# A hybrid decoder layer: each piece of side work is queued on ScalarE and VectorE behind the split of the weights beside it

## The chip, the cores and the metric

The kernel runs on one core of one Trainium2 chip. The metric is the device time of one execution in microseconds (us). The time before is the median of three executions. A profile of one further execution gives the rows that are read below. Engines are named as in the profile: PE is TensorE, ACT is ScalarE, DVE is VectorE, POOL is GpSimd, SP is SyncE, whose queue issues most of the DMAs. L268 is line 268 of the kernel.

## What is computed

One layer of a decoder on 512 tokens of width 1024, all in float32. After a modulated norm, three mixers (a Mamba-2 state space mixer called SSD, dilated window attention, and pooling over windows) are projected, gated, summed and projected again. An MLP with squared ReLU follows. Both have gated residuals. Cut to its frame:

```python
mod = (cond @ w_ada[l] + b_ada[l])[:, None, :]
sh1, sc1, g1, sh2, sc2, g2 = jnp.split(mod, 6, axis=-1)
h = _rms(x, norm1_w[l]) * (1 + sc1) + sh1
x = x + g1 * _hybrid_mixer(h, ...)
h = _rms(x, norm2_w[l]) * (1 + sc2) + sh2
x = x + g2 * (jnp.square(jax.nn.relu(h @ w_ff1[l])) @ w_ff2[l])
# in the mixer
z, xbc, dt_raw, q, k, v, u, gates = jnp.split(h @ w_in, splits, axis=-1)
# in _ssd, per head: the decay between two tokens of a chunk of 128
seg = a_cum[:, :, :, None] - a_cum[:, :, None, :]
decay = jnp.exp(jnp.where(causal, seg, -jnp.inf))
y_diag = jnp.einsum('bclsgj,bcsgjp->bclgjp', cb[..., None] * decay, X)
```

## The kernel before

*The stream of weights.* Each projection is a loop over tiles of weights, 128 x 1024 (two blocks of 128 rows of K, 512 KB). `wstream` loads a tile by a DMA on SP into `raw`. `wsplit` then makes two parts of it for float32 accuracy: ACT copies it to `wh` in a rounded format, DVE subtracts and keeps the rest in `wl`. `mm3` multiplies three times (L282 and L283 with wh, L284 with wl), for four accumulators `psacc` and two blocks, so a tile feeds 24 matmuls of 512 columns. `raw` has four buffers, `wh` and `wl` three each. Load and split are traced with high priority, 300 places ahead.

*Side work.* Everything that is not such a projection is cut into pieces. After each tile `tick()` takes one piece from the list `side`, and as many as `st["pace"]` says from the list `background`. Pieces of `side` are parts of the attention (scores, softmax, transposes: psqT, qT, pskT, kT, psS, p), of the SSD mixer (`ssd_steps`, `ssd_heads`), of the pooling (`win`, `pd`, psmix). `background` holds 32 pieces of `ada_later`: each loads a tile of `w_ada` on SP (wada, L243), multiplies and sums it on DVE (L244) and adds a bias (L245), for the later parts of `mod`. The pace is 0 until the loop over `w_ssd_out`, 2 there for its first round, then 1; the loads take one of four buffers in turn.

*Decay tiles.* For each pair of heads `ssd_heads` fetches two rows of `prow` into tiles `M`, spread over all partitions, by a DMA on SP (L899). Then come on ACT an exponential for `e` (L904), on DVE L911 or on ACT L909 the subtraction with a ReLU, on ACT the exponential L912, on DVE the product with `cb` (L913). In a later piece PE multiplies them into `psy` (L919), and DVE adds (L922, L928 to L933). Between the ReLU and exponentials on the one side and the SiLU of `conv` (L839) and of `z` (L321) or the square roots (L197) on the other, ACT loads a table.

*The order.* From L329 on, the instructions of DVE, ACT, PE and SP are put in order by a scheduler from the code's order and priorities, and by when it reckons that their inputs are ready. The order that comes out is fixed when the kernel is built. An engine then runs its own queue in that order and waits wherever an instruction's inputs are not there. `tc.issue_after(ins)` is a rule for the scheduler: what is traced within it comes, on the engine of `ins`, behind `ins`. It adds no wait between engines.

*PSUM.* Accumulators take banks that other results leave. The fourth accumulator of `take_x(1)` (psacc_3040, the XS projection of the second SSD group) gets the bank of `psst`, the state of an SSD chunk, which ACT copies to `prev` (L882). Copies of `z` (L321) come beside it.

Of the kernel before, what the change touches and what calls it, by code (L numbers as in the profile page):

```python
# [10 lines left out]
F32 = mybir.dt.float32  # L11
F32R = mybir.dt.float32r
AF = mybir.ActivationFunctionType
ALU = mybir.AluOpType
# [84 lines left out]
def kernel(ctx: ExitStack, tc: tile.TileContext, a: dict, out: bass.AP, dbg=None):  # L99
# [13 lines left out]
    def uid(s):  # L113
        cnt[0] += 1
        return f"{s}_{cnt[0]}"
# [47 lines left out]
    V, S = nc.vector, nc.scalar  # L163
# [75 lines left out]
    def ada_later(part, k):  # L239
        def go():  # L240
            o = modv[:, part - 2, k : k + 1]
            w = exp.tile([P, 2, T], F32, tag=("L0", "L1", "N0", "N1")[k % 4], name=uid("wada"))
            nc.sync.dma_start(w, a["w_ada"][part * 8 + k].rearrange("p (i t) -> p i t", i=2))  # L243
            V.scalar_tensor_tensor(w, w, 1.0, crow2, ALU.mult, ALU.mult, accum_out=o)  # L244
            V.tensor_tensor(o, o, vc("b_ada", part * 8 + k), ALU.add)  # L245
        return go


    background = [ada_later(part, k) for part in (2, 3, 4, 5) for k in range(8)]
    side, st = [], {}  # L250

    def tick():
        if side:
            side.pop(0)()
        for f in background[: st.get("pace", 0)]:
            f()
        del background[: st.get("pace", 0)]

    def flush():
        while side:  # L260
# [3 lines left out]
    def wsplit(raw, shape):  # L264
        wh = wsp.tile(shape, F32R, tag="wh", name=uid("wh"))
        wl = wsp.tile(shape, F32R, tag="wl", name=uid("wl"))
        S.copy(wh, raw)  # L267
        V.tensor_tensor(wl, raw, wh.bitcast(F32), ALU.subtract)  # L268
        return wh, wl

    def wstream(w, nk, ch, k0=0, ahead=None):
        for kp in range(nk // 2):
            with tc.high_priority(offset=AHEAD if ahead is None else ahead):
                raw = raws.tile([P, 2, T], F32, tag="raw", name=uid("raw"))
                nc.sync.dma_start(raw, w[ch, k0 // 2 + kp])
                wh, wl = wsplit(raw, [P, 2, T])
            for i in range(2):
                yield 2 * kp + i, wh[:, i, :], wl[:, i, :]
            tick()
# [696 lines left out]
    def pool_mix(gi):  # L976
        raw = raws.tile([P, 2, 256], F32, tag="raw", name=uid("wmix"))
        nc.sync.dma_start(raw, a["w_pool_mix"][gi])
        wh, wl = wsplit(raw, [P, 2, 256])
        for m in range(2):  # L980
            ps = psm("mix")
            cs = slice(m * P, (m + 1) * P)
            for k in range(2):
                mm3(ps, wh[:, k, cs], wl[:, k, cs], dh[2 * gi + k], dl[2 * gi + k], k == 0, k == 1)
            x, y = blk("poolh", F32R), blk("pooll", F32R)
            S.activation(x, ps, AF.Copy, scale=vc("pool_scale", gi * 2 + m))
            V.scalar_tensor_tensor(y, ps, vc("pool_scale", gi * 2 + m), x.bitcast(F32), ALU.mult, ALU.subtract)
            free(ps)
            ph_.append(x)
            pl_.append(y)  # L990
        free(*dh[2 * gi : 2 * gi + 2], *dl[2 * gi : 2 * gi + 2])
# [481 lines left out]
```

## Time and profile before

| | |
|---|---|
| median of 3 executions | 1100.88 us (1098.8 to 1102.0) |
| profiled execution | 1100.18 us, of which the span of the instructions 1098.4 us |
| mean granted TensorE clock | 0.998 |
| instructions | 14808 |
| read from HBM | 130.89 MB, 121 GB/s read and written over the span |

Busy time is counted per engine over the span. Engines work side by side, and PE is the one that is almost never idle; so the rows to read are those in which PE waits, with the engine that releases it, and then what that engine did before. A row of the timeline has the start, the duration, the engine, the line and the operation with its tiles, and in brackets the idle time ahead of it and who ended it. A row of groups has count, busy time, mean in ns, idle time ahead.

### The profile page before, as it was taken

Reading aid. Unit: us, or ns where it says so; the run is one execution under the profiler, and the core shown is the slowest. Engines: PE = TensorE matmul, PEld = TensorE weight load, DVE = VectorE, ACT = ScalarE, POOL = GpSimd, SP = SyncE. Lnnn points to the kernel's source line nnn. Section 1 sums busy time; section 2 is a strip of 40 time slices with the busy share of each in tenths; the row PEclk is TensorE's granted clock in tenths of the full one; section 3 lists DMA queues with packets and bytes.
Section 4 is the critical chain, followed back from the end, with each engine's and each line's share of the span. In section 5 each row is a group of like instructions: output and inputs, shape, how many; then the busy total and the mean of one; then the engine's idle time right before and its main releaser. Section 6 shows DMA issues by size and latency. Waiting matters only on the chain.

```text
span 1098.4 us, 14808 instructions
## 1 busy us (share of the span) xinstructions
PE 1087.7 (99%) x5806; PEld 928.4 (85%) x5806; DVE 709.0 (65%) x1287; ACT 520.2 (47%) x839; POOL 3.6 (0%) x10
## 2 busy tenths in 40 slices
PE   8999999999999999999999999999999999999998
PEld 7878888888887888887888888899889989989987
DVE  7955744461574658499984424477787587686664
ACT  8965865543793456424532123354344334334330
POOL 0000000000000000000000000000000000000000
PEclk9999999999999999999999999999999999999999
DMA  9823223222432233384283334260214234134032
GB/s 337 307 96 93 69 76 112 75 78 77 134 96 87 77 121 111 126 317 157 91 324 123 106 97 163 96 230 1 77 58 151 61 97 135 59 114 135 20 116 76
DMA packets 42057, 133.97 MB, mean 122 GB/s; under 512 B 4850, under 2 KB 5618, under 8 KB 41988
## 3 DMA queue, kind: packets, MB, share of 16 engines
q1 hardware_dynamic: 40784, 130.28, 35.8%
q0 software_dynamic: 480, 1.57, 0.5%
q10 hardware_dynamic: 724, 1.18, 0.3%
q8 instruction: 45, 0.74, 0.3%
q14 instruction: 24, 0.20, 0.1%
HBM read 130.89 MB, written 2.13 MB: 121 GB/s over the span
## 4 chain that ended last, share of the span: by engine, by line
PE 89%; DVE 5%; ACT 3%; DMA 2%; issue 1%; SPq 0%; DVEq 0%; ACTq 0%
PE psacc L282 22%; PE psacc L284 22%; PE psacc L283 22%; PE psacc L1334 11%; PE psacc L522 4%; PE psS L601 1%; DMA wada<-in_w_ada_dram 1%; DVE conv L837 1%; DMA M<-prow 1%; DVE win L964 1%; DVE wl L268 1%; PE pspT L698 1%; PE pskT L585 0%; PE pso L717 0%; PE psqT L580 0%
## 5 line engine op out<-in xcount | busy, mean ns | idle before, releaser
L268 DVE TENSOR_TENSOR wl<-raw,wh 128x1024 fp32r<-128x1024 f32 x140 | 171.0, 1223 | 206.0 <-ACT wh L267 205.6
L267 ACT CAST wh<-raw 128x1024 fp32r<-128x1024 f32 x140 | 146.6, 1048 | 264.9 <-PE psacc L283 192.5
L282 PE MATMUL psacc<-hl,wh 128*128 128x512 f32 x416 | 167.4, 402 | 3.1 <-ACT prev L882 2.0
L283 PE MATMUL psacc<-hh,wh 128*128 128x512 f32 x416 | 162.7, 391 | 0.0
L284 PE MATMUL psacc<-hh,wl 128*128 128x512 f32 x416 | 162.0, 391 | 0.0
L282 PE MATMUL psacc<-al,wh 128*128 128x512 f32 (+1 forms) x260 | 100.4, 386 | 0.0
L283 PE MATMUL psacc<-ah,wh 128*128 128x512 f32 (+1 forms) x260 | 100.4, 386 | 0.0
L284 PE MATMUL psacc<-ah,wl 128*128 128x512 f32 (+1 forms) x260 | 100.3, 386 | 0.0
L282 PEld LDWEIGHTS psacc<-hl,wh 128*128 128x128 f32 x416 | 78.6, 189 | 21.0 <-ACT prev L882 2.4
L283 PEld LDWEIGHTS psacc<-hh,wh 128*128 128x128 f32 x416 | 78.7, 189 | 17.0 <-issue 1.4
L284 PEld LDWEIGHTS psacc<-hh,wl 128*128 128x128 f32 x416 | 78.5, 189 | 16.9
L282 PE MATMUL psacc<-wl,rh 128*128 128x512 f32 x192 | 77.0, 402 | 0.0
L283 PE MATMUL psacc<-wh,rh 128*128 128x512 f32 x192 | 75.4, 393 | 0.0
L284 PE MATMUL psacc<-wh,rl 128*128 128x512 f32 x192 | 75.4, 393 | 0.0
L284 PEld LDWEIGHTS psacc<-ah,wl 128*128 128x128 f32 x260 | 48.8, 188 | 9.9
L282 PEld LDWEIGHTS psacc<-al,wh 128*128 128x128 f32 x260 | 48.9, 188 | 9.7
L283 PEld LDWEIGHTS psacc<-ah,wh 128*128 128x128 f32 x260 | 48.9, 188 | 9.6
L1394 DVE SCALAR_TENSOR_TENSOR xr<-psacc,modv,xr 128x512 f32<-128x512 f32 (+1 forms) x65 | 44.8, 741 | 18.7 <-PE psacc L284 18.7
L244 DVE SCALAR_TENSOR_TENSOR wada<-wada,crow 128x1024 f32<-128x1024 f32 x32 | 38.8, 1221 | 6.0 <-DMA wada<-in_w_ada_dram 6.0
L284 PEld LDWEIGHTS psacc<-wh,rl 128*128 128x128 f32 x192 | 36.1, 188 | 7.6
L282 PEld LDWEIGHTS psacc<-wl,rh 128*128 128x128 f32 x192 | 36.0, 188 | 7.2 <-ACT qT L581 0.2
L283 PEld LDWEIGHTS psacc<-wh,rh 128*128 128x128 f32 x192 | 36.1, 188 | 6.8
(407 smaller groups left out, 2344.2 us busy)
## 6 DMA issues: line engine op xcount, KB each, us to landing
raw<-in_w_in_dram SPq DMA_DIRECT2D x80, 512.0 KB, 3.5
raw<-in_w_ff_dram SPq DMA_DIRECT2D x52, 512.0 KB, 3.9
wada<-in_w_ada_dram SPq DMA_DIRECT2D x46, 512.0 KB, 5.1
rawl<-in_w_ff_dram SPq DMA_DIRECT2D x12, 512.0 KB, 3.4
wst<-in_w_in_dram SPq DMA_DIRECT2D x16, 256.0 KB, 7.8
M<-prow SPq DMA_DIRECT2D x16, 256.0 KB, 4.2
raw<-in_w_ssd_out_dram SPq DMA_DIRECT2D x8, 512.0 KB, 3.6
raw<-in_w_pool_out_dram SPq DMA_DIRECT2D x8, 512.0 KB, 3.5
```

The source lines that it names most:

```text
L244: V.scalar_tensor_tensor(w, w, 1.0, crow2, ALU.mult, ALU.mult, accum_out=o)
L267: S.copy(wh, raw)
L268: V.tensor_tensor(wl, raw, wh.bitcast(F32), ALU.subtract)
L282: mm(ps, lhsT=wh, rhs=xl, start=first, stop=False)
L283: mm(ps, lhsT=wh, rhs=xh, start=False, stop=False)
L284: mm(ps, lhsT=wl, rhs=xh, start=False, stop=last)
L522: mm(ps[j], lhsT=t[:, j, :], rhs=w, start=first, stop=last)
L601: mm(so[b], lhsT=qT[:, b * P : (b + 1) * P], rhs=kT[:, (b + 1) * P - n : (b + 1) * P], start=True, stop=True)
L698: nc.tensor.transpose(tp[:, i : i + P], pt[half][:, i : i + P], ident)
L837: V.scalar_tensor_tensor(t[:, i:], x[:, : T - i], cw[:, 3 - i, n : n + 1], t[:, i:], ALU.mult, ALU.add)
L1334: mm(o, lhsT=x[:, cs], rhs=y, start=first and k == 0 and j == 0 and n == 0, stop=k == 3 and n == 2, skip_group_check=True)
L1394: V.scalar_tensor_tensor(xT[d][:, ts], p[:, : ts.stop - ts.start], modv[:, 3, d : d + 1], xT[d][:, ts], ALU.mult, ALU.add)
```

## The change

`wsplit` now keeps in `edges` the two instructions of the latest split, the copy on ACT and the subtraction on DVE. `tick` traces its pieces within `issue_after` of both: on ACT they come behind the wh, on DVE behind the wl of the tile that was traced just before. What the pieces issue on PE and SP is not bound by this, except through the order that the scheduler finds. Pieces that `flush` runs are not bound. The decay rows are still loaded on SP's queue.

```diff
-    side, st = [], {}
+    side, st, edges = [], {}, []
 
     def tick():
-        if side:
-            side.pop(0)()
-        for f in background[: st.get("pace", 0)]:
-            f()
-        del background[: st.get("pace", 0)]
+        fs = side[:1] + background[: st.get("pace", 0)]
+        del side[:1], background[: st.get("pace", 0)]
+
+        with tc.issue_after(edges[0].ins), tc.issue_after(edges[1].ins):
+            for f in fs:
+                f()
...
-        S.copy(wh, raw)
-        V.tensor_tensor(wl, raw, wh.bitcast(F32), ALU.subtract)
+        edges[:] = S.copy(wh, raw), V.tensor_tensor(wl, raw, wh.bitcast(F32), ALU.subtract)
```

The split stands at L267 and L268 before, at L268 after. What moves, at three places:

ACT around the copies of z and prev, before. M_3374, M_3375 and M_4019 are decay tiles, the last one of the second SSD group:

```order
L912 ACTIVATE M_3374<-M_3374 128x512
L909 ACTIVATE M_3375<-M_3375,npc_939 128x128 x4
L912 ACTIVATE M_3375<-M_3375 128x512
L267 CAST wh_3087<-raw_3085 128x1024
L909 ACTIVATE M_4019<-M_4019,npc_939 128x128
L321 ACT_TABLE_LOAD
L321 ACTIVATE z_3029<-psacc_2869 128x512
L267 CAST wh_3129<-raw_3127 128x1024
L321 ACTIVATE z_3030<-psacc_2870 128x512
L321 ACTIVATE z_3031<-psacc_2871 128x512
L882 COPY prev_3027<-psst_3025 128x512
L321 ACTIVATE z_3032<-psacc_2872 128x512
```

and after, on the same engine:

```order
L268 CAST wh_3043<-raw_3041 128x1024
L851 COPY Bt_2933<-psBt_2935 128x512
L268 CAST wh_3087<-raw_3085 128x1024
L321 ACTIVATE z_3029<-psacc_2869 128x512
L321 ACTIVATE z_3030<-psacc_2870 128x512
L321 ACTIVATE z_3031<-psacc_2871 128x512
L268 CAST wh_3129<-raw_3127 128x1024
L321 ACTIVATE z_3032<-psacc_2872 128x512
L882 COPY prev_3027<-psst_3025 128x512
```

The decay tiles and the table load have gone from here: the first ones come behind wh_3229, two tiles later, and M_4019 in the next group's turn. On SP the DMA of M_4019 has moved from behind raw_3227 to behind raw_3736.

DVE between two products of psy (conv_3211 and conv_3217 are two of the SSD's outputs, wl_4384 the split of a tile of the pooling projection), one piece of the difference:

```order
 L268 TENSOR_TENSOR wl_4384<-raw_4381,wh_4383 128x1024
-L232 TENSOR_TENSOR sums_4111<-sums_4111,sq_4179 128x512
 L922 SCALAR_TENSOR_TENSOR conv_3211<-conv_3211,dcol_93,psy_4227 128x512
 L928 TENSOR_TENSOR e_4147<-psyo_4237,e_4147 128x384
-L245 TENSOR_TENSOR modv_94<-modv_94,vec_79 128x1
-L244 SCALAR_TENSOR_TENSOR wada_5139,modv_94<-wada_5139,crow_81 128x1024
 L930 TENSOR_TENSOR conv_3211<-conv_3211,e_4147 128x384
+L933 TENSOR_TENSOR conv_3211<-conv_3211,z_3480 128x512
```

The wada work has left this place; its first reduction (wada_4873) now stands right behind wl_4846, the first tile of `w_ssd_out`, and the last of the 32 follows one or two at a time behind later tiles.

ACT in the attention, before (qT_1232 and kT_1233 are the transposed q and k of one head, p_1177 and p_1178 the probabilities of the head before, rkr a root of the norm of k):

```order
L544 ACTIVATE sq_1215<-k_1200 128x512
L581 COPY qT_1232<-psqT_1234 128x512
L586 ACTIVATE kT_1233<-pskT_1240,qkw_282 128x512
L616 ACTIVATE p_1177,zs_182_748<-p_1177,nmx_749 128x128
L616 ACTIVATE p_1177,zs_182_748<-p_1177,nmx_749 128x256
L616 ACTIVATE p_1178,zs_182_748<-p_1178,nmx_749 128x256 x2
L197 ACT_TABLE_LOAD
L197 ACTIVATE rkr_1219<-ssk_1205,epsc_91 128x16
```

and after:

```order
L544 ACTIVATE sq_1215<-k_1200 128x512
L616 ACTIVATE p_1177,zs_182_748<-p_1177,nmx_749 128x128
L616 ACTIVATE p_1177,zs_182_748<-p_1177,nmx_749 128x256
L616 ACTIVATE p_1178,zs_182_748<-p_1178,nmx_749 128x256 x2
L197 ACT_TABLE_LOAD
L197 ACTIVATE rkr_1219<-ssk_1205,epsc_91 128x16
L581 COPY qT_1232<-psqT_1234 128x512
L586 ACTIVATE kT_1233<-pskT_1240,qkw_282 128x512
```

The two copies stand behind the exponentials and the root. PE has, ahead of the accumulator psacc_1291 that needs their banks, 18 matmuls of 512 columns and four transposes more than before.

## The prediction

> **What bounds the kernel now.** I read the busy shares first, then the waits of TensorE (PE), then the stretches around each wait.
>
> The first table of the page, and after it the list of what PE waited for (total, times, longest, us):
>
> ```profile
> PE 1087.7 (99%) x5806; PEld 928.4 (85%) x5806; DVE 709.0 (65%) x1287; ACT 520.2 (47%) x839; POOL 3.6 (0%) x10
> ```
> ```profile
> PE psacc L282 <- ACT prev L882: 2.0, 1, 2.0
> ...
> PE psacc L282 <- DVE conv L922: 0.9, 1, 0.9
> PE psmix L284 <- DVE wl L268: 0.4, 1, 0.4
> ```
>
> PE is busy 99% of 1098.4 us. The change adds and removes no matmul, so it can give back only PE's waits and what follows them. These three are the waits behind streamed weights; the list's others lie in the opening or are shorter, and no order changes there. Around the first, PE in order of time (start, duration):
>
> ```profile
> 333.78 0.38 PE L867 MATMUL psX<-cst,conv 128*128 128x128 f32 x2
> 334.00 1.02 PE L878 MATMUL psst<-Xd,Bt 128*128 128x512 f32 x2
> ...
> 336.47 0.39 PE L283 MATMUL psacc<-hh,wh 128*128 128x512 f32 x1
> 336.70 0.39 PE L284 MATMUL psacc<-hh,wl 128*128 128x512 f32 x1
> 339.11 0.79 PE L282 MATMUL psacc<-hl,wh 128*128 128x512 f32 x1 [2.02 <-ACT prev L882]
> ...
> 342.61 0.40 PE L284 MATMUL psacc<-hh,wl 128*128 128x512 f32 x1
> ```
> and the same time in windows (length; busy time of PE, PEld, DVE, ACT, POOL; granted clock, DMA share, GB/s):
> ```profile
> 336.90:339.10 2.20, 0.19 (x1) 0.00 (x0) 1.47 (x2) 2.20 (x5) 0.00 (x0) 1.00 0.00 0
> 339.10:342.50 3.40, 3.39 (x8) 2.72 (x9) 0.96 (x2) 0.46 (x1) 0.00 (x0) 0.50 0.48 154
> ```
>
> Full-speed matmuls start 0.23 us apart (336.47 to 336.70; 0.227 over longer rows of them). The gap from 336.70 to 339.11 is 2.41, so 2.18 too long. Then the granted clock is 0.50 for 3.4 us: eight intervals from 339.11 to 342.61 take 3.50 where 8 x 0.227 = 1.82 would do, 1.68 more. This one wait cost 3.86 us, twice what the list of waits shows.
>
> Why prev was late stands on ACT, with the DMA that it waited for:
>
> ```profile
> 330.85 0.33 SPq L899 DMA_DIRECT2D M<-prow  x1
> ```
> ```profile
> 334.35 0.40 ACT L909 ACTIVATE M<-M,npc 128x128 f32<-128x128 f32 x1 [3.32 <-DMA M<-prow]
> 334.77 1.28 ACT L321 ACT_TABLE_LOAD   x1
> 336.06 0.60 ACT L321 ACTIVATE z<-psacc 128x512 f32<-128x512 f32 x1
> 336.56 1.04 ACT L267 CAST wh<-raw 128x1024 fp32r<-128x1024 f32 x1
> 337.49 1.09 ACT L321 ACTIVATE z<-psacc 128x512 f32<-128x512 f32 x2
> 338.46 0.60 ACT L882 COPY prev<-psst 128x512 f32<-128x512 f32 x1
> ```
>
> A relu of the next group's decay tile (M_4019) had been put ahead of z and prev. Its row was fetched only at 330.85, so ACT stood 3.32 us, then loaded a table for 1.28, and prev ended at 339.06. PE's fourth accumulator needs the bank that prev reads. That piece of side work, pulled ahead of the main path, is what the change forbids.
>
> **The change, part by part.**
>
> *First wait.* In the new order ACT has, after the Bt copy, wh_3087, three z, wh_3129, the fourth z and prev, with no decay work and no table load between. PE finished the last z bank before its L867 of 333.78, so wh_3129 and the fourth z can run from there: 1.04 (the wh of 336.56), z 0.60 and prev 0.60, each overlapping the next by some 0.1, end near 335.8. prev also needs PE's psst, done at 335.02, which allows that. PE wants the bank at 336.70 + 0.23 = 336.93, 1.1 us later. I take the whole wait as gone, and the slow clock with it: **-3.86**. The bounds are 0, if something else holds ACT there, and -3.86.
>
> *Second and third waits.* On PE, on ACT (one wh) and on DVE:
>
> ```profile
> 497.62 0.39 PE L283 MATMUL psacc<-hh,wh 128*128 128x512 f32 x1
> 498.94 0.51 PE L282 MATMUL psacc<-hl,wh 128*128 128x512 f32 x1 [0.94 <-DVE conv L922]
> ...
> 535.36 0.50 PE L284 MATMUL psmix<-pdh,wl 128*128 128x512 f32 x1 [0.40 <-DVE wl L268]
> ```
> ```profile
> 493.44 1.05 ACT L267 CAST wh<-raw 128x1024 fp32r<-128x1024 f32 x1
> ```
> ```profile
> 498.14 0.75 DVE L922 SCALAR_TENSOR_TENSOR conv<-conv,dcol,psy 128x512 f32<-128x512 f32 x1
> ...
> 534.62 0.68 DVE L268 TENSOR_TENSOR wl<-wmix,wh 128x512 fp32r<-128x512 f32 x1
> ```
>
> 498.94 - 497.62 = 1.32, less 0.23, is 1.09 lost; here the clock stays. DVE's groups from 466 to 498.2 say who is in the way, and the windows how full it is:
>
> ```profile
> L244 DVE SCALAR_TENSOR_TENSOR wada<-wada,crow 128x1024 f32<-128x1024 f32 x11 | 13.4, 1223 | 2.4 <-DMA wada<-in_w_ada_dram 2.4
> L268 DVE TENSOR_TENSOR wl<-raw,wh 128x1024 fp32r<-128x1024 f32 x5 | 6.1, 1222 | 0.0
> ```
> ```profile
> 283.00:340.00 57.00, 54.98 (x264) 45.62 (x263) 39.90 (x64) 51.80 (x82) 0.00 (x0) 0.99 0.38 112
> 340.00:466.00 126.00, 126.00 (x621) 102.14 (x621) 74.26 (x119) 59.71 (x91) 0.00 (x0) 0.99 0.33 107
> 466.00:536.00 70.00, 68.67 (x364) 55.70 (x363) 67.03 (x150) 24.77 (x35) 0.00 (x0) 1.00 0.55 188
> 536.00:640.00 104.00, 104.00 (x461) 86.12 (x460) 63.77 (x106) 33.48 (x42) 0.00 (x0) 1.00 0.53 178
> ```
>
> DVE is busy 67.0 of 70 us from 466 to 536, and eleven wada reductions with their loads took 13.4 + 2.4 = 15.8 of the 32 us until the wait. All these now stand behind a split of w_ssd_out or later, after 540. The scheduler fills part of the room with pooling work, and conv L922 stays behind wl_4431, whose wh comes only when PE frees its slot. By the rows: wh ends at 494.49, a pooling add of 0.69 may be under way until 495.1, wl 1.22 and L922 0.75 less the overlap give 497.0; PE, which has three matmuls fewer ahead of that bank, arrives 0.68 earlier than 497.62 + 0.23, at 497.2. I take **-0.9** of 1.09 (bounds 0 and -1.09). The third wait lost 0.4 in the list and, with the slowed intervals beside it, up to 0.67. wl_4662 now comes some 3 us earlier on DVE, but PE too asks earlier, since fewer matmuls are put ahead of psmix L284: ready 531.6, asked 531.6, by the same kind of sum, no better than 1 us either way. I take **-0.4** (bounds +0.3 and -0.67).
>
> *Where the moved work goes.* The decay tiles leave 283 to 340 (ACT 51.8 of 57 busy) for 352 to 388, in the stretch with ACT 59.7 of 126 and DVE 74.3 of 126. psy needs the first and the third pair at (PE, then two wh on ACT):
>
> ```profile
> 374.17 1.09 PE L919 MATMUL psy<-M,X 128*64 128x128 f32 x16
> ...
> 388.92 1.09 PE L919 MATMUL psy<-M,X 128*64 128x128 f32 x16
> ```
> ```profile
> 350.98 1.05 ACT L267 CAST wh<-raw 128x1024 fp32r<-128x1024 f32 x1 [5.73 <-PE psacc L283]
> ...
> 381.42 1.04 ACT L267 CAST wh<-raw 128x1024 fp32r<-128x1024 f32 x1 [1.77 <-PE psacc L283]
> ```
> The pieces start on ACT behind the wh of 350.98 and, with the row durations of 0.39 to 0.63 an activation and 1.28 a table load, I get the first pair ready at 357.5, needed at 374.2; the third, behind the wh of 381.42, at 383.2, needed at 388.9, the tightest of the four. Cover 5.7 us: **0**. If it is gone, psy is late next. The 32 wada loads and reductions spread over 540 to 690, two for each weight tile of 24 x 0.227 = 5.45 us of PE. DVE has 63.8 of 104 busy there including 15 of them. A tile then asks DVE for 1.22 + 2 x (1.22 + 0.15) = 4.0 of 5.45, and wl is finished one or two tiles before PE asks: **0**. On SP's queue a wada load behind a raw load can wait for its slot and hold the next raw, which has four buffers ahead: **0**. POOL's queue is unchanged.
>
> *In attention*, at 116 to 125, side work gave way to other orders: the copies qT_1232 and kT_1233 stand behind four exponentials, a table load and a square root instead of before them.
>
> ```profile
> 118.90 0.60 ACT L581 COPY qT<-psqT 128x512 f32<-128x512 f32 x1
> 119.36 0.72 ACT L586 ACTIVATE kT<-pskT,qkw 128x512 f32<-128x512 f32 x1
> ...
> 122.30 1.28 ACT L197 ACT_TABLE_LOAD   x1
> 123.59 0.31 ACT L197 ACTIVATE rkr<-ssk,epsc 128x16 f32<-128x16 f32 x1
> ```
> I get them at 124.1 and 124.7. PE has 18 wide matmuls more ahead of them (18 x 0.227 = 4.1 us) and four transposes, and asks at 124.3 and 125.0 where it asked at 119.92. The margin is 0.2: bounds 0 and +1.3 (one table load), taken **+0.2**. Other places where orders changed (a da chain at 88 us, a bank at 392) have margins of 0.3 to 0.5 and may cost as much: together **+0.3**, bounds 0 and +1.
>
> [...]
>
> Sum: -3.86 - 0.9 - 0.4 + 0.2 + 0.3 = **-4.7**. The profiled execution took 1100.18 (span 1098.4 and 1.8 around it), so 1095.5 on its scale; the median of the runs shown is 1100.88, 0.7 higher. I take **1096.0**, between 1095.5 and 1096.2.
>
> **The rivals.** *Only the first wait goes.* Then -3.86 and +0.5: 1097.1 to 1097.5, about 1097.3. For it: both later waits are on DVE with margins of 0.2 or none. Against: eleven reductions leave.
>
> *New waits in attention or at a bank eat the gain.* A wait of 2 us, as at 336.7, costs 3.9 with its clock: 1096.0 + 3.9 = 1099.9, the same within the measurement (0.3%, 3.3 us, is about the least that timing tells from no change). For it: margins of 0.2 to 0.5 us. Against: the wait must pass about 1 us before the clock falls, since after the 0.94 at 498.94 it did not.
>
> *The slow clock stays.* If the 0.50 at 339.1 had another cause than the wait, 1.68 stays: 1097.7. [...] The trace shows the fall right behind 2.2 us idle, and nowhere else in this stretch.
>
> *Slower: the decay tiles come late.* Their pieces sit in ACT's order behind a wh that itself waits for PE (1.77 at 381.42). If the third pair is over 5.7 us later than I sum, PE waits at psy, at 388.9, and the fourth pair follows. At 3 us each with 1.7 of slow clock that is 9.4: 1096.0 + 9.4 = 1105.4. For it: extra table loads between z's silu and relu and exp. Against: ACT and DVE are half empty there.
>
> *The change does not bind here*, since a scheduler puts other work ahead of prev: 1100.9. The order shows prev without such work, so this is small.
>
> **How the numbers follow.** Forecast 0.57 (1094.8 to 1097.2); only the first wait 0.13; slow clock stays 0.05; attention or a bank 0.12; no effect 0.05; slower 0.08. Faster by over 0.3% means under 1097.6: the first, most of the second and half of the third, 0.70. Slower, above 1104.2: 0.08. The rest, 0.22. The range reaches from 1094.0 (all bounds at their best, -5.6, with 0.5 of scatter) to 1099.9, where the slower case and the unchanged one are left out.
>
> **What would show it.** Right: no PE wait on prev L882 and a clock of 1.00 around 339; PE's total of waits on conv L922 and wl L268 under 0.4; no relu of M between 283 and 340; wada reductions up to about 690 us without PE waits on wl. Wrong: a PE wait on qT L581 or kT L586 near 124, on M L913 at psy, or another window with clock 0.50.

## The result, and the profile after

The change makes the kernel faster by about half a per cent: 1093.55 us in the median (1093.37 to 1094.08, 6 executions) against 1099.59 of the kernel before beside it (1096.67 to 1102.0, 6), a ratio of 0.9945 with a 95% interval of 0.9930 to 0.9961. The profiled execution took 1093.54 with a span of 1091.7 and a mean granted clock of 1.0. Forecast were 1096.0 and a range of 1094.0 to 1099.9: the sign was right, and the time lies 0.45 below the range. One later execution of the kernel before, in the third group below, took 1819.69 us at a mean clock of 0.556 and is left out of all figures.

The page after, PE's busy time and the chain that ended last (shares of the span by engine), and then all that PE waited for (total, times, longest, us):

```profile
PE 1085.3 (99%) x5806; PEld 927.7 (85%) x5806; DVE 711.9 (65%) x1287; ACT 514.9 (47%) x835; POOL 3.6 (0%) x10
...
PE 98%; DVE 1%; DMA 0%; issue 0%; ACT 0%; SPq 0%; DVEq 0%
```
```profile
PE pssx L400 <- DVE sq L409: 1.3, 1, 1.3
PE pswarm L393 <- DVE ones L362: 1.1, 1, 1.1
PE psrx L454 <- DVE diag L451: 0.3, 1, 0.3
```

The list of waits no longer has prev, conv and wl; the three that are left lie in the opening. The stretches of the prediction, after (length; busy time of PE, PEld, DVE, ACT, POOL; clock, DMA share, GB/s):

```profile
283.00:340.00 57.00, 57.00 (x278) 47.55 (x277) 31.92 (x41) 28.57 (x41) 0.00 (x0) 1.00 0.35 116
340.00:466.00 126.00, 126.00 (x625) 102.23 (x624) 81.32 (x141) 79.24 (x129) 0.00 (x0) 1.00 0.36 115
466.00:536.00 70.00, 70.00 (x371) 57.38 (x370) 57.88 (x119) 29.04 (x43) 0.00 (x0) 1.00 0.23 74
536.00:640.00 104.00, 104.00 (x461) 86.11 (x460) 71.58 (x124) 31.74 (x39) 0.00 (x0) 1.00 0.71 242
```

PE is busy all the time in all four. ACT fell from 51.8 to 28.6 us in the first and rose from 59.7 to 79.2 in the second: the decay tiles moved. DVE fell from 67.0 to 57.9 in the third and rose by 7.8 in the fourth: the wada work moved. At the first of the old waits, on ACT and then on PE:

```profile
332.60 1.04 ACT L268 CAST wh<-raw 128x1024 fp32r<-128x1024 f32 x1
333.55 0.59 ACT L321 ACTIVATE z<-psacc 128x512 f32<-128x512 f32 x1
334.08 0.59 ACT L882 COPY prev<-psst 128x512 f32<-128x512 f32 x1
```
```profile
335.94 0.39 PE L282 MATMUL psacc<-hl,wh 128*128 128x512 f32 x1
336.16 0.39 PE L283 MATMUL psacc<-hh,wh 128*128 128x512 f32 x1
```

prev ends at 334.67 and PE starts into that bank at 335.94, 1.27 us later, at full pace. At the second, DVE's addition and PE's first matmul into the bank, and at the third, DVE's split and PE's psmix:

```profile
491.18 0.74 DVE L922 SCALAR_TENSOR_TENSOR conv<-conv,dcol,psy 128x512 f32<-128x512 f32 x1
...
525.66 0.69 DVE L268 TENSOR_TENSOR wl<-wmix,wh 128x512 fp32r<-128x512 f32 x1
```
```profile
492.27 0.40 PE L282 MATMUL psacc<-hl,wh 128*128 128x512 f32 x1
...
526.55 0.40 PE L284 MATMUL psmix<-pdh,wl 128*128 128x512 f32 x1
```

L922 ends at 491.92, 0.35 before PE asks; wl ends at 526.35, 0.20 before. So the last two are met with little to spare.

To see where the time came from, the start of PE's k-th matmul was set against the k-th of the kernel before (both have 5806), at points where the order of the matmuls is the same in both. The differences, added up to some points of the kernel before:

| up to, us before | after minus before, us | this part |
|---|---|---|
| 20 (opening) | -0.57 | -0.57 |
| 116 | -0.47 | +0.10 |
| 220 (attention) | -0.94 | -0.47 |
| 296 | -0.98 | -0.04 |
| 348 (first wait) | -4.90 | -3.92 |
| 497 | -4.89 | 0.0 |
| 503 (second wait) | -6.16 | -1.27 |
| 543 (third wait) | -6.66 | -0.50 |
| end | -6.65 | 0.0 |

Nothing was given back after 116; the 0.10 up to there comes at 88 to 96, beside the da chain that the prediction names.

### The profile page after: what moved, and what is told of

Its sections match the earlier page's. It is cut to its first block, busy times and chain, and to the rows that moved or that the text cites. A ratio compares the mean times of both kernels' runs of the same rounds, so it can differ in the third digit from the quotient of the medians.

```text
span 1091.7 us, 14800 instructions
## 1 busy us (share of the span) xinstructions
PE 1085.3 (99%) x5806; PEld 927.7 (85%) x5806; DVE 711.9 (65%) x1287; ACT 514.9 (47%) x835; POOL 3.6 (0%) x10
## 3 DMA queue, kind: packets, MB, share of 16 engines
HBM read 130.89 MB, written 2.13 MB: 122 GB/s over the span
## 4 chain that ended last, share of the span: by engine, by line
PE 98%; DVE 1%; DMA 0%; issue 0%; ACT 0%; SPq 0%; DVEq 0%
PE psacc L282 25%; PE psacc L284 25%; PE psacc L283 25%; PE psacc L1334 11%; PE psacc L522 4%; PE psS L601 1%; PE psy L919 1%; PE pso L717 1%; PE psyo L927 1%; PE pspT L698 1%; PE pso L715 1%; PE psqT L580 0%; PE pskT L585 0%; PE psst L878 0%; DMA xT<-in_x_dram 0%; PE psmix L284 0%
## 5 line engine op out<-in xcount | busy, mean ns | idle before, releaser
L268 DVE TENSOR_TENSOR wl<-raw,wh 128x1024 fp32r<-128x1024 f32 x140 | 171.1, 1222 | 191.8 <-ACT wh L268 189.2
L268 ACT CAST wh<-raw 128x1024 fp32r<-128x1024 f32 x140 | 146.8, 1050 | 275.5 <-PE psacc L283 176.5
L1334 PE MATMUL psacc<-gh,wl 128*128 128x256 f32 x144 | 40.8, 283 | 0.0
```

The lines of the kernel that those rows point to most:

```text
L268: edges[:] = S.copy(wh, raw), V.tensor_tensor(wl, raw, wh.bitcast(F32), ALU.subtract)
L1334: mm(o, lhsT=x[:, cs], rhs=y, start=first and k == 0 and j == 0 and n == 0, stop=k == 3 and n == 2, skip_group_check=True)
```

## The experiments

The account to be tested: what stops PE is side work that stands in ACT's and DVE's order ahead of main work. On ACT it is the ReLU behind the late row M; on DVE it is the wada reductions. The rivals are that the relief comes from fewer table loads and less work on ACT, or that the slow clock is no result of the wait. Edits are to the kernel after. All times of a group come from one chip with runs of the kernel before beside them.

**One edge at a time.** First group: the kernel before took 1097.82 (1096.37 to 1099.6, 19 executions).

```diff
-        with tc.issue_after(edges[0].ins), tc.issue_after(edges[1].ins):
+        with tc.issue_after(edges[0].ins):   # e1: behind wh on ACT only
+        with tc.issue_after(edges[1].ins):   # e2: behind wl on DVE only
```

> The pieces are held behind the wh on ACT only, not behind the wl on DVE. The order on ACT at z and prev is that of the changed kernel, but eleven or so wada reductions stay on DVE ahead of conv L922. My account (three separate waits): the wait on prev with its slow clock is gone (-3.9 of the 6.0 us), the waits of DVE (1.3 and 0.5) may stay, so 1 to 2 us above the changed kernel: 1094.6 to 1095.4. Rival (DVE's queue is what matters): prev is late again or other waits of 2 us come, 1097 or more.

With ACT's edge alone: 1094.24 (1093.96 to 1094.64), ratio 0.9965 (0.9952 to 0.9978). That is 0.4 below the expected band: the wait for prev is gone, and so is the one for conv, which the expectation had let stay, though wada reductions still run on DVE from 465.8 (9 between 455 and 498 where the kernel before has 12). Only the third is left, PE's row:

```profile
529.36 0.50 PE L284 MATMUL psmix<-pdh,wl 128*128 128x512 f32 x1 [0.58 <-DVE wl L268]
```

> The pieces are held behind the wl on DVE only. On ACT decay work stays among z and conv, with 37 rows of table loads where the kernel before has 30 and the changed one 26; but the ReLU of M_4019 is gone from ahead of z, and wada is gone from DVE. My account: all three waits gone, within 0.5 us of the changed kernel: 1093.5 to 1094.1. Rival (the gain is ACT's saved table loads and load on ACT, 5 us fewer): 7 more loads of 1.28 make ACT late for z, prev or wh, 1097 to 1100.

With DVE's edge alone: 1094.49 (1093.97 to 1094.68), ratio 0.9963 (0.9950 to 0.9976), and no wait of PE after the opening. The median lies 0.4 above the end of the expected band; in the trace, the kernel after is ahead by 0.46 in the opening and by 0.38 between there and 220. ACT in this kernel, where decay work and table loads have stayed:

```profile
324.85 1.28 ACT L912 ACT_TABLE_LOAD   x1
326.15 0.63 ACT L912 ACTIVATE M<-M 128x512 f32<-128x512 f32 x1
327.56 1.05 ACT L268 CAST wh<-raw 128x1024 fp32r<-128x1024 f32 x1 [0.78 <-PE psacc L283]
328.62 1.28 ACT L321 ACT_TABLE_LOAD   x1
...
335.38 0.59 ACT L882 COPY prev<-psst 128x512 f32<-128x512 f32 x1
```
and the window over it:
```profile
283.00:340.00 57.00, 57.00 (x276) 47.53 (x275) 32.08 (x40) 49.23 (x77) 0.00 (x0) 1.00 0.39 116
```

ACT is busy 49.2 of 57 us, nearly as before (51.8), and prev is in time. So the table loads and the amount of work on ACT were not the cause; what is gone from here is the ReLU that waited for its row. Either edge alone gives most of the gain. That a decay piece uses both engines, so that one bound instruction puts the piece off, would explain it, but no run takes this apart.

**One kind of side work at a time.** In the same group:

```diff
-        fs = side[:1] + background[: st.get("pace", 0)]
+        fs, bs = side[:1], background[: st.get("pace", 0)]   # e4: only wada bound
...
+        for f in fs:
+            f()
         with tc.issue_after(edges[0].ins), tc.issue_after(edges[1].ins):
-            for f in fs:
+            for f in bs:
                 f()
```

> Only the background pieces (wada) are held, the side work is free as before. My account: the waits on conv L922 and wl L268 go (1.3 + 0.5), that on prev with its slow clock stays: 1.7 us below the kernel before, about 1098, with a PE wait on prev of about 2 us and a granted clock of 0.5 behind it. Rival (the first wait is also fed by DVE's crowding): the wait on prev shrinks, 1096 or less.

1096.08 (1095.78 to 1098.74, 10 executions), ratio 0.9987 (0.9978 to 0.9997). The wait for prev is back, those for conv and wl are not: the sums of differences fall by 1.26 and 0.50 across them, as in the whole change, and DVE is busy 20.0 of the 32 us from 466 to 498 (29.6 before). So binding the wada work alone takes away the second and third wait. The wait for prev, the windows on it, and one in the opening:

```profile
PE psacc L284 <- ACT prev L884: 1.6, 1, 1.6
```
```profile
10.00:15.00 5.00, 5.00 (x29) 5.00 (x29) 3.65 (x14) 2.60 (x6) 0.00 (x0) 0.59 1.04 365
...
338.70:340.70 2.00, 0.41 (x3) 0.03 (x1) 1.51 (x2) 2.00 (x5) 0.00 (x0) 1.00 0.00 0
340.70:344.20 3.50, 3.50 (x15) 2.85 (x16) 0.92 (x2) 0.45 (x2) 0.00 (x0) 1.00 0.44 150
```

After this wait of 1.59 the clock stays at 1.00. The profiled execution (1098.41) lost its 2 us in the opening instead, where the clock fell to 0.59; seven of the ten executions, with a clock of 0.999 and above, took 1095.8 to 1096.2. The 1098 that was expected counted on the slow clock and was missed; the time is near the rival's. But the wait is only 0.4 shorter than in the first profile, and in the kernel before no wada reduction runs on DVE between 52 and 463 us, so these can't have fed a wait at 337.

The other way round, only the decay pieces of the second SSD group are bound (e5):

```diff
-        side.append(lambda: next(gens[0]))
+        side.append(bind(lambda: next(gens[0])))   # bound only if g == 1
...
-            side.append(go)
+            side.append(bind(go))
```

> Only the decay pieces of the second SSD group are held; on ACT the one difference at prev is that the ReLU of M_4019 no longer stands ahead of z. My account (that one instruction, which waits for its DMA, makes the whole first loss): -3.9 us against the kernel before, 1095.5 to 1096, no PE wait on prev, waits on DVE as before. Rival (decay work of the first group and its table loads on ACT between 283 and 340 make prev late as well): a wait of 1 us or more on prev stays, 1097 to 1099.

1095.33 (1095.03 to 1097.16, 8), ratio 0.9976 (0.9966 to 0.9986). ACT, where the first group's decay work stands as before, but the ReLU of the second group doesn't stand ahead of z:

```profile
328.70 0.63 ACT L911 ACTIVATE M<-M 128x512 f32<-128x512 f32 x1
329.24 1.04 ACT L267 CAST wh<-raw 128x1024 fp32r<-128x1024 f32 x1
330.29 1.28 ACT L320 ACT_TABLE_LOAD   x1
...
334.72 0.59 ACT L881 COPY prev<-psst 128x512 f32<-128x512 f32 x1
```
and PE at the third wait:
```profile
530.22 0.50 PE L283 MATMUL psmix<-pdh,wl 128*128 128x512 f32 x1 [0.82 <-DVE wl L267]
```

Binding these pieces alone takes away the first wait: the sums of differences go from -0.73 to -4.65 across it, as in the whole change. The second wait went too, against the expectation and though the wada work is not bound. DVE has 8 reductions there instead of 12 between 455 and 498, the last at 485.8 where the kernel before has one at 492.8; later decay work seems to have taken their turns. It is no less busy for it (31.7 of the 32 us from 466 to 498; in e1, where the wait is gone as well, 31.5; before 29.6). The third wait grew to 0.82. So the first wait belongs to the pieces of this group, of which one ReLU stood ahead of z. The second and third go with the wada work by e4; in e1 and e5 the second hangs on which work has DVE's turns just ahead of L922, and not on how busy DVE is.

**Both kernels again, and the slow clock.** Second group, another chip: the kernel before took 1097.74 (1095.84 to 1101.27, 28 executions).

> The changed kernel once more, beside many executions of the kernel before on one chip. Account as it stands after the first four experiments: without the slow clock the first wait costs some 2, the others 1.3 and 0.5, attention 0.4, so 4.2 us between the medians (ratio 0.996). Rival (the 6.0 us of the first comparison is the usual gain, the slow clock usual too): ratio 0.9945.

The unchanged kernel after: 1093.51 (1093.3 to 1093.97, 6), ratio 0.9962 (0.9949 to 0.9975). That is the 4.2 us of the account, and the interval leaves out the rival's 0.9945.

> The kernel before once more, for a second profile of it and its scatter. If the slow clock behind the wait on prev is a matter of chance, most executions have a mean granted clock of 1.000 and lie within about 1 us of each other, and those with 0.998 or less lie about 1.7 us above them. If it always follows the wait, all have 0.998. Ratio 1.000.

The unchanged kernel before: 1097.82 (1096.69 to 1101.84, 10), ratio 0.9999 (0.9986 to 1.0011). Eight executions have a mean clock of 0.999 or above and lie between 1096.7 and 1097.9; two have less and took 1099.38 and 1101.84. The profiled one is the slowest. PE at both waits, and the windows:

```profile
336.05 0.39 PE L284 MATMUL psacc<-hh,wl 128*128 128x512 f32 x1
338.29 0.50 PE L282 MATMUL psacc<-hl,wh 128*128 128x512 f32 x1 [1.84 <-ACT prev L882]
...
499.05 0.65 PE L282 MATMUL psacc<-hl,wh 128*128 128x512 f32 x1 [1.82 <-DVE conv L922]
```
```profile
338.30:342.00 3.70, 3.70 (x10) 2.90 (x11) 0.93 (x2) 0.43 (x1) 0.00 (x0) 0.57 0.46 142
...
500.00:503.00 3.00, 3.00 (x9) 2.37 (x8) 3.00 (x8) 1.25 (x2) 0.00 (x0) 0.56 0.02 5
```
and DVE's addition:
```profile
498.25 0.74 DVE L922 SCALAR_TENSOR_TENSOR conv<-conv,dcol,psy 128x512 f32<-128x512 f32 x1
```

Here the clock fell behind both waits. L922 ends at 498.99, in the first profile at 498.89, although PE came 0.8 us earlier: DVE's own queue, with the wada loads that it waits for, sets that time in this kernel, so what PE had gained upstream came back as wait. Of 65 executions of the kernel before in the three groups, 10 show a mean clock of 0.998 or less, and they are its ten slowest (1099.35 and above); the twelve executions of the kernel after all show 1.0 and keep within 0.8 us. Both profiles of before fell on such executions. A usual one was not profiled, so what its waits look like was not seen.

To measure how long a wait brings the clock down, dummy activations that switch tables were put ahead of prev in the kernel after, and later matmuls were kept from filling the gap (`end` holds the last matmul of the projection's first block):

```diff
                     if d == 0:
+                        for f in (AF.Exp, AF.Sqrt) * 2 if g == 0 else ():   # e6_tables6: * 3
+                            S.activation(pv[:, :1], sp[:, :1], f, scale=0.0)
                         S.copy(pv, sp)
...
+                    if ch == XS + 1 and k:
+                        es.enter_context(tc.issue_after(end[0].ins))
```

> The changed kernel with four extra one-column activations, each with a table load, on ACT ahead of the copy to prev, and with PE kept from taking the second block's matmuls of that projection before the fourth accumulator's first ones. prev is then some 5.9 us later; less 1.3 to spare and 1.9 of other matmuls put between, PE waits about 2.7. If the clock falls behind every wait of 2 us or more: about 4.4 above the changed kernel in every execution. If it falls by chance: 2.7 in some, 4.4 in others. [...]

1095.62 (1095.54 to 1095.97, 10), ratio 0.9982 (0.9973 to 0.9992), 2.1 over the kernel after. ACT, PE, and the window behind:

```profile
338.16 0.17 ACT L888 ACTIVATE prev<-psst 128x1 f32<-128x1 f32 x1
338.35 1.28 ACT L888 ACT_TABLE_LOAD   x1
339.64 0.17 ACT L888 ACTIVATE prev<-psst 128x1 f32<-128x1 f32 x1
```
```profile
340.49 0.50 PE L282 MATMUL psacc<-hl,wh 128*128 128x512 f32 x1 [1.51 <-ACT prev L889]
```
```profile
340.00:344.00 4.00, 3.51 (x15) 2.92 (x16) 2.76 (x4) 0.44 (x2) 0.00 (x0) 1.00 0.00 0
```

The wait is 1.51, where 2.7 was expected, so this run doesn't test a wait of 2 us. It leaves the clock at 1.00, in all ten executions (0.999 and above).

> The same with six such activations: a PE wait of about 5.7. [...] If the clock is a matter of chance even here, some executions at 5.7.

1100.72 (1100.04 to 1104.66, 10), ratio 1.0033 (1.0021 to 1.0044), 7.2 over the kernel after. PE's wait, and the window behind it:

```profile
343.76 0.71 PE L282 MATMUL psacc<-hl,wh 128*128 128x512 f32 x1 [4.47 <-ACT prev L889]
```
```profile
343.70:347.20 3.50, 3.44 (x8) 2.72 (x9) 2.76 (x4) 0.01 (x1) 0.00 (x0) 0.53 0.00 0
```

A wait of 4.47 (5.7 was expected) brings the clock to 0.53 for 3.5 us, and all ten executions show a mean clock of 0.998 or less. Two more table switches, 2 x 1.48 = 2.96 us by the rows above (338.16 to 339.64), cost 1100.72 - 1095.62 = 5.1: the window has eight matmuls in 3.5 us, like the eight intervals of 3.50 that the prediction read behind the wait for prev, so the clock adds some 1.7 by that estimate, and 0.4 stays unexplained. So with the same neighbours a wait of 1.51 leaves the clock at 1.00, and one of 4.47 brings it down to 0.53.

**Attention, and the spread of wada.** Third group: the kernel before took 1097.82 (1096.68 to 1100.74, 8 executions). Here the binding begins with the SSD part, after the attention (e9):

```diff
-        with tc.issue_after(edges[0].ins), tc.issue_after(edges[1].ins):
+        with ExitStack() as es:
+            for e in edges if st.get("bind") else ():
+                es.enter_context(tc.issue_after(e.ins))
...
+    st["bind"] = True
     ps = evac(gemm_feat(w_in, 8, BCC, hh, hl), "xc")
```

> The changed kernel, with pieces held only from the first projection of the SSD mixer (BCC) on; in the attention the old order stands. Account: all of the gain but the 0.4 us that four profiles with held side work show between 116 and 217 us: 1093.9, no PE wait after the opening. Rival (those 0.4 come from chance, as in the opening): 1093.5. Rival (the attention needs the rule): a wait there, over 1095.

1093.82 (1093.72 to 1093.98, 5), ratio 0.9958 (0.9943 to 0.9973). In its trace the part from 116 to 220 us differs from before by 0.0, where the whole change shows -0.47, and the 0.10 at 88 is not there either; the waits are gone as in the whole change. The attention was thus a small gain of the change and not the cost that the prediction took. The median agrees in size, 0.3 over the kernel after's, but that is of another chip and within what the intervals leave open.

The last one lets the wada work run twice as dense where it went (e8):

```diff
-        st["pace"] = 2
+        st["pace"] = 4
```

> The changed kernel with four background pieces behind each tile of w_ssd_out instead of two. A tile then asks DVE for 1.22 + 4 x 1.37 = 6.7 us where PE takes 5.45, and four buffers of loads that land in some 5 us each allow no more than four pieces in 6.5. Account (wl has some 8 us of cover): four tiles fall behind by 4 to 5 us in all, no PE wait, 1093.5. Rival (there was little cover, and the pace of two was just enough): PE waits on wl L268 of 2 us or more, 1096 or above.

1093.28 (1092.99 to 1094.06, 5), ratio 0.9953 (0.9935 to 0.9971). The reductions in this kernel (count, least, median and most ns, first and last start) and what ended DVE's idle time ahead of them (us, times):

```profile
L244 DVE SCALAR_TENSOR_TENSOR wada<-wada,crow x32: 1217/1220/1227, 543.5 to 616.4; 128x1024 f32<-128x1024 f32 x32
...
  DMA wada<-in_w_ada_dram: 6.5, 7
```

In 73 us instead of the 121 of the kernel after, with DVE now waiting 6.5 us for loads instead of 0.9, and still PE waits for no wl. So the cover that the prediction counted for the moved wada work is there. This version is not measurably faster than the kernel after.

## Why the prediction was right, and where it was not

The mechanism held: all three waits went, the first for the reason argued, the others with the wada work. The forecast of the time did not: 1093.55 lies below the range. The step that failed is the low end of the range, which took as the best case of each place what a single gap of the profile showed, and 0 where it showed none: attention gave 0.47 where 0 was the best, the second wait 1.27 where 1.09 was. A further 0.57 is the opening of the profiled execution, from which everything was subtracted.

*The first wait* came out as argued: forecast -3.86 with 1.1 us to spare, measured -3.92 with 1.27. The cause was shown in four ways: the wait goes with the second group's pieces alone (e5), it goes with a busy ACT and its table loads in place (e2), it stays when only wada is bound (e4), and a wait of 4.47 made by other means has a slow clock behind it too, 0.53 (e6_tables6).

*The second wait* was taken at -0.9 with 1.09 as the most; it gave -1.27, with a spare time of 0.35 where 0.2 was reckoned. Its bound was too small: it counted the one gap of 498.94 and not the slowed matmuls behind it (0.51 us for the first instead of 0.39), as the first wait's term had done. *The third* was taken at -0.4 and gave -0.50, within its bounds. That these two go with the wada work on DVE, as argued, is what e4 shows; but e1 and e5 lost the second with 9 and 8 reductions still ahead of it, so that all eleven had to leave was not needed.

*Attention and the other places* are where the step failed most. They were given +0.2 and +0.3, with 0 as the best end. No reason excluded a gain there, and the attention gave -0.47, the others together +0.08 (+0.10 of them at the da chain at 88). The new order had qT and kT ready in time, ACT and PE after:

```profile
121.36 1.28 ACT L197 ACT_TABLE_LOAD   x1
...
123.34 0.69 ACT L586 ACTIVATE kT<-pskT,qkw 128x512 f32<-128x512 f32 x1
```
```profile
124.50 0.82 PE L601 MATMUL psS<-kT,qT 128*128 128x128 f32 x4
```

kT ends at 124.03, 0.47 before PE starts psS, which waits for nothing. The list of waits has none there before, but half of the gain stands at one place: before, psmzN (L642) starts 0.37 behind the matmul ahead of it (216.85 to 217.22), after 0.23 (216.14 to 216.37), and it runs 0.08 shorter. The rest lies between 116 and 130, where the order of the matmuls differs, and was not traced to one instruction. The gain shows in the five other traces with the attention bound on ACT (the kernel after again, e1, e8 and both e6), and in none of those where it is not (e4, e5, e9, the kernel before again) or where only DVE's edge holds (e2).

*The sum.* -4.66 was forecast, before rounding, and -6.65 measured, trace against trace. Of the 1.99 between, attention is 0.67, the other places 0.22, the second wait 0.37, the third 0.10, the first 0.06, and 0.57 lies in the opening, which the change does not touch up to some 62 us and which differs by +1.96 to -0.9 among the other traces: chance. Then 0.5 was added to come nearer to the median of the runs shown. Together that is the 2.45 by which 1096.0 is too high. The gain has another error, which leaves the time after as it is: the profile of before is of the rarer kind with the slow clock, so 1.7 of its -3.86 is there in a part of the executions only. In the second group the medians differ by 1097.74 - 1093.51 = 4.2, in the first comparison by 6.0. That the -4.7 lies between is luck: terms that were too small stand against a slow clock that is rarely there.

*The rivals.* Only the first wait goes: no, all three do. The slow clock stays: no, it went with the wait (1.00 in the four windows after). New waits in attention or at a bank: none. Decay tiles late: psy, from 369.3, waits for nothing, with ACT's decay work from 347. No effect: no. All the signs that were named for a right forecast are there; only the last wada reduction starts at 664.6, where about 690 was reckoned.

## What to carry to other kernels

Look at what stands in an engine's order ahead of an instruction that frees a bank of the bound engine, and above all for side work whose input comes by a late DMA: here the 3.32 us that ACT stood behind a row fetched late, with z and prev behind it in its order, cost 3.9 on PE, and the decay pieces of one group put behind the split beside them gave them back. Look also for a wait whose end is set by another engine's own queue: in the repeat of the kernel before the second wait swallowed 0.8 us gained upstream. And in summing up such a change, price each touched place from both sides, and ask whether the profiled execution is a usual one: here it held 1.7 us of slow clock that most executions don't have.

## What the runs showed of the hardware

In dense rows of matmuls PE's clock stayed at 1.00 behind idle times of 0.94 (first profile of before, 499 to 502), 1.51 (e6_tables4) and 1.59 us (e4). Behind 1.82 and 1.84 (second profile of before), 2.02 (first profile) and 4.47 (e6_tables6) the windows of 3.0 to 3.7 us show it at 0.50 to 0.57; behind the 2.02 that cost 1.68 more. The prediction's "about 1 us" was too low: 1.51 and 1.59 left the clock where it was.

The length alone did not decide it, though. In the opening of the first profile of before, PE waited 2.28 us, longer than the 2.02 at prev, and the window behind it shows the full clock:

```profile
9.02 1.05 PE L400 MATMUL pssx<-ones,sq 128*128 128x1 f32 x8 [2.28 <-DVE sq L409]
```
```profile
9.10:12.50 3.40, 3.40 (x30) 3.35 (x31) 3.19 (x8) 3.11 (x5) 0.00 (x0) 1.00 1.01 361
```

In the opening of e4 PE waited 2.13 us ahead of the same matmuls (pssx at 8.62), and the window from 10 to 15 shows 0.59. What decides beside the length was not shown.

In e6_tables4 a table load with its one-column activation took 1.48 us (338.16 to 339.64), and the activation started 0.01 us after the end of the load's 1.28 (338.35 to 339.63). So did z in the first profile of before, at 336.06 after the load of 334.77 + 1.28 = 336.05.

The scatter of the kernel before (1095.8 to 1101.8 over the three groups) shrank to 1093.3 to 1094.1 with the waits gone. The clock makes a part of it: the 55 executions at a mean clock of 0.999 and above still spread from 1095.8 to 1099.3. What spreads these was not traced; a wait of 1.51 made by dummies on ACT (e6_tables4) did not, with 1095.5 to 1096.0.
